# Small unused tiles in front of the activation tiles, hi and lo halves joined

## The chip, the cores and the metric

The kernel runs on one core of a Trainium2 chip. The metric is the device time of one execution in microseconds: 1652.95 us, the median of 3 runs (1650.94 to 1655.68).

## The reference

Two blocks are applied to x, 256 positions by 1024 channels, all in float32. The first has two layers. Each layer is a half-weighted SwiGLU FFN, a mixer, and a second such FFN:

```python
for l in range(DEPTH):                                   # DEPTH = 2
    x = x + 0.5 * swiglu(rms_norm(x, ffn1_norm[l]), ffn1_w_gate_up[l], ffn1_w_down[l])
    u = rms_norm(x, mix_norm[l]) @ w_in[l]
    y = concatenate([ssd_mixer(u_ssd), mlstm_mixer(u_ml), rwkv7_mixer(u_rw)])
    x = x + y @ w_out[l]
    x = x + 0.5 * swiglu(rms_norm(x, ffn2_norm[l]), ffn2_w_gate_up[l], ffn2_w_down[l])
return rms_norm(x, final_norm)
```

The hidden width of an FFN is 2816. The second block has one layer: attention of 8 heads with a distance bias beside a short convolution, an output projection, and a fifth FFN of the same size with a three-tap convolution on its up projection; six modulation vectors come from a 1024 x 6144 product with a condition vector (the "ada" weights).

## The kernel before

Channels lie on the partitions, positions along them: an activation is a tile of [128, 8, 256] (8 blocks of 128 channels, 256 positions each). A weight matrix is cut into blocks of 128 x 128; 7 blocks are one chunk of 448 KB in the order in which they are used. `fetch` (line 120) brings a chunk into `raw` through SyncE's DMA queue, six ahead. `chunk` (lines 125 to 135) splits it: ScalarE casts it to float32r (`whi`, line 133) and VectorE subtracts (`wlo`, line 134); four chunks of each are held. Activations are split in the same way (`split`, lines 203 to 205). So one float32 block product is three matmuls of 256 columns, hi x hi, hi x lo, lo x hi (`mm`, lines 150 to 154), summed in a PSUM bank `d`:

```python
PE.matmul(p, h, xh, ...)      # line 152
PE.matmul(p, h, xl, ...)      # line 153
PE.matmul(p, lo, xh, ...)     # line 154
```

The first argument after `p` is the 128 x 128 weight block, which TensorE loads; the second is the activation, which streams through it. There are 3808 blocks, 11424 such matmuls.

The stages run in this order: FFN, mixers, FFN in layer 0; the same in layer 1; attention and fifth FFN. In an FFN the up projection (`group`, `dense2`: 8 blocks per result) reads `xn`, the normalised x, and the down projection (22 blocks per result) reads the hidden tiles `hh` and `hl`. The first four results of an up projection, the "lead", read `xg` instead, x times the gain without the normalisation, so that TensorE has work while the statistic is computed (sum on TensorE, line 220; root on GpSimd, line 211; spread over partitions on TensorE, line 249). In the mixers the input projections read `xn` and a planner (`weave`) puts the chains of the three mixers between them in a fixed order; then `w_out` reads their results `y`. TensorE, ScalarE, VectorE and GpSimd each work in the order of the program.

The tiles that matter here come from pools. `big` (line 255) is [128, 8, 256], 8192 bytes of each partition, four buffers: `xg`, `xn`, the SSD part's inputs and its result each take two of them, one for hi and one for lo. The small results of the mixers take [128, 2, 256] tiles `w2` of a ring. The hidden tiles `hh` and `hl` (lines 314, 315) are the first large tiles of a pool per FFN. Where a tile begins follows from what was allocated before it. In the built program, before and after the change, the tiles begin at these byte offsets of a partition, modulo 512 (one weight block is 512 bytes, one activation block 1024). The weights, `whi` and `wlo`, begin at 416 in every buffer and every block, before and after. The columns d give the activation's offset minus 416, modulo 512.

| moving operand | matmuls | offset before | d before | offset after | d after |
|---|---|---|---|---|---|
| `xn` of five FFNs | 4800 | 416 | 0 | 96 | 192 |
| `xn` and SSD result in two mixers | 2160 | 416 | 0 | 96 | 192 |
| `xg`, six leads | 576 | 416 | 0 | 352 | 448 |
| `xn` of the attention | 480 | 416 | 0 | 352 | 448 |
| mixers' `y` in `w2` tiles | 384 | 192 | 288 | 96 | 192 |
| hidden, FFN 1 of layer 0 | 528 | 96 | 192 | 96 | 192 |
| hidden, FFN 2 of layer 0 | 528 | 96 | 192 | 352 | 448 |
| hidden, FFN 1 of layer 1 | 528 | 96 | 192 | 160 | 256 |
| hidden, FFN 2 of layer 1 | 528 | 224 | 320 | 32 | 128 |
| hidden, fifth FFN | 528 | 224 | 320 | 288 | 384 |
| `mixed` of the attention | 192 | 224 | 320 | 96 | 192 |
| `xgh` and `xgl`, two leads of 258 columns | 192 | 96, 160 and on in steps of 8 | 192, 256 and on | 224, 288 and on | 320, 384 and on |

Of the kernel before, what the change touches and what calls it, by code (L numbers as in the profile page):

```python
# [16 lines left out]
T = 256  # L17
# [22 lines left out]
DENSE = 0.34  # L40
W_OUT = ((("rwkv0", "rwkv1"), (12, 13, 14, 15)), (("ssd",), (0, 1, 2, 3, 4, 5, 6, 7)), (("mlstm",), (8, 9, 10, 11)))
# [35 lines left out]
def _program(tc, a, order, dbg=None):  # L77
# [91 lines left out]
    def group(mat, l, ms, K, xs, lead):  # L169
        pp = [bank(), bank()]  # L170

        def step(i, m, k):
            mm(pp[i // 2][:, i % 2], (mat, l, k, m), xs[0][:, k], xs[1][:, k], k == 0 and i % 2 == 0, k == K - 1)
# [107 lines left out]

    OUTS = ((0, 1), (2, 3), (4, 5), (6,), (7,))
# [4 lines left out]
    def gained(js, xg, gain):  # L287
        col = [P(gain, j) if isinstance(gain, str) else gain[:, j:j + 1] for j in js]
        for j, c in zip(js, col):
            S.activation(xg[0][:, j, :T], x[:, j], AF.Copy, scale=c)  # L290
        for j, c in zip(js, col):
            V.scalar_tensor_tensor(xg[1][:, j, :T], x[:, j], c, xg[0][:, j, :T].bitcast(F32),
# [7 lines left out]
    def normalize(rb, gain):  # L300
        xn = pair()
        for j in range(0, DT, 2):
# [3 lines left out]
            split(n, xn[0][:, j:j + 2], xn[1][:, j:j + 2])  # L306
        return xn

    def ffn(l, which, acc, xg, next_gain):
        with tc.tile_pool(name=f"ffn{which}{l}", bufs=1) as fp:  # L310
            gu, dn = f"ffn{which}_w_gate_up", f"ffn{which}_w_down"
            rb, = stat_rstd([acc], D, EPS)
            xn = normalize(rb, f"ffn{which}_norm{l}")
            hh = fp.tile([128, FT, T], F32R, name="hh")
            hl = fp.tile([128, FT, T], F32R, name="hl")
            groups = ADA[2 * l + which - 1]
            n_ada = 8 * len(groups)
            for t in range(FT):
# [15 lines left out]
                split(h, hh[:, t], hl[:, t])  # L334
# [16 lines left out]
            for js in OUTS:  # L351
                p = dense2(dn, l, js, FT, (hh, hl))[:, :len(js)]
# [20 lines left out]
    def mixers(l, acc, xg):  # L373
# [10 lines left out]

        nka = mp.tile([128, 4], F32, name="nka")
# [30 lines left out]
        def w_in(name):  # L416
# [37 lines left out]
        def w_out(js, ks, last):  # L454
            p = bank()[:, :len(js)]
            for u, j in enumerate(js):
                for i, k in enumerate(ks):
                    hi, lo = b["y", k]
                    mm(p[:, u], ("w_out", l, k, j), hi, lo, i == 0, i == len(ks) - 1)
# [1025 lines left out]
```

## Time and profile before

| what | value |
|---|---|
| median of 3 runs | 1652.95 us (1650.94 to 1655.68) |
| the profiled execution: span from first to last instruction | 1648.7 us |
| TensorE matmul / weight load busy | 1606.0 us (97%) / 1540.1 us (93%) |
| VectorE / ScalarE / GpSimd busy | 1162.8 us (71%) / 1001.7 us (61%) / 46.3 us (3%) |
| read from HBM | 287.51 MB, 175 GB/s over the span |

Matmuls are pipelined, so the busy time of TensorE counts overlapping instructions once and says little of its pace; the distance between the starts of two matmuls (here: the pitch) is read from the timeline, or from the count of matmuls in a stretch. A line such as `d<-big,whi` gives the output tile, then the inputs by the program's names without buffer numbers. An activation is named there by its pool's name: `big` is `xn` or `xg` or the SSD result, `w` is a tile of the ring `w2`.

### The profile page before, as it was taken

How to read it: one execution, taken by the hardware profiler on the slowest of the kernel's cores; microseconds unless marked ns; L12 is line 12 of the kernel's file. 1: busy time of each engine (PE TensorE's matmuls, PEld its weight loads, DVE VectorE, ACT ScalarE, POOL GpSimd, SP SyncE). 2: the span in 40 equal slices, each digit the busy share in tenths (PEclk: the TensorE clock that was granted, in tenths of full speed). 3: DMA queues.
4: the chain of work that ended last, by engine and by line, in shares of the span. 5: the costliest groups of instructions: out<-in, count | busy, mean ns of one | idle time of the engine just before them, and what ended most of it. 6: DMA issues, size and time to landing. Idle time of an engine off the chain costs nothing.

```text
span 1648.7 us, 33731 instructions
## 1 busy us (share of the span) xinstructions
PE 1606.0 (97%) x13660; PEld 1540.1 (93%) x13660; DVE 1162.8 (71%) x1961; ACT 1001.7 (61%) x1688; POOL 46.3 (3%) x58
## 2 busy tenths in 40 slices
PE   8999999999999999999999899999999999999998
PEld 7999988877999999999998887899999998999997
DVE  7755689856877655777568975588785676698863
ACT  6444586887655444544457788766544566477753
POOL 0000001000000000000000100000000000000000
PEclk9999999999999999999999999999999999999999
DMA  7855643334357656597563333435885553455562
GB/s 257 291 182 188 200 128 123 104 116 125 112 175 253 212 181 194 180 328 241 183 200 126 123 102 106 129 126 200 290 294 180 185 163 112 146 165 183 184 195 73
DMA packets 106717, 290.81 MB, mean 176 GB/s; under 512 B 15640, under 2 KB 28096, under 8 KB 106432
## 3 DMA queue, kind: packets, MB, share of 16 engines
q1 hardware_dynamic: 106272, 288.12, 53.7%
q8 instruction: 107, 1.75, 0.4%
q10 hardware_dynamic: 288, 0.52, 0.1%
q14 instruction: 50, 0.41, 0.1%
HBM read 287.51 MB, written 1.09 MB: 175 GB/s over the span
## 4 chain that ended last, share of the span: by engine, by line
PE 80%; issue 13%; ACT 3%; DVE 3%; POOL 1%; DMA 0%; DVEq 0%; POOLq 0%; SPq 0%; ACTq 0%
PE d L154 22%; PE d L153 22%; PE d L152 22%; PE m L680 1%; POOL stm L211 1%; PE m L743 1%; PE m L1055 1%; ACT whi L133 1%; PE m L1059 1%; PE m L725 1%; DVE wlo L134 1%; PE st L220 1%; PE m L694 1%; PE m L1057 1%; PE m L590 0%
## 5 line engine op out<-in xcount | busy, mean ns | idle before, releaser
L134 DVE TENSOR_TENSOR wlo<-raw,whi 128x896 fp32r<-128x896 f32 x544 | 590.9, 1089 | 266.8 <-ACT whi L133 264.7
L152 PE MATMUL d<-big,whi 128*128 128x256 f32 x2672 | 761.6, 285 | 3.6 <-ACT whi L133 2.2
L154 PE MATMUL d<-big,wlo 128*128 128x256 f32 x2672 | 762.1, 285 | 1.8 <-DVE wlo L134 1.8
L153 PE MATMUL d<-big,whi 128*128 128x256 f32 x2672 | 762.4, 285 | 0.2
L133 ACT CAST whi<-raw 128x896 fp32r<-128x896 f32 x544 | 511.3, 942 | 389.2 <-PE d L153 281.4
L152 PEld LDWEIGHTS d<-big,whi 128*128 128x128 f32 x2672 | 512.8, 192 | 12.8 <-issue 6.3
L154 PEld LDWEIGHTS d<-big,wlo 128*128 128x128 f32 x2672 | 512.6, 192 | 6.8 <-issue 2.5
L153 PEld LDWEIGHTS d<-big,whi 128*128 128x128 f32 x2672 | 512.9, 192 | 3.8 <-issue 1.7
L153 PE MATMUL d<-hl,whi 128*128 128x256 f32 x880 | 244.5, 278 | 0.0
L152 PE MATMUL d<-hh,whi 128*128 128x256 f32 x880 | 244.1, 277 | 0.0
L154 PE MATMUL d<-hh,wlo 128*128 128x256 f32 x880 | 243.8, 277 | 0.0
L154 PEld LDWEIGHTS d<-hh,wlo 128*128 128x128 f32 x880 | 165.2, 188 | 0.0
L152 PEld LDWEIGHTS d<-hh,whi 128*128 128x128 f32 x880 | 165.2, 188 | 0.0
L153 PEld LDWEIGHTS d<-hl,whi 128*128 128x128 f32 x880 | 165.1, 188 | 0.0
L204 ACT CAST hh<-h 128x256 fp32r<-128x256 f32 x88 | 35.4, 406 | 71.0 <-DVE h L333 71.0
L1115 DVE SCALAR_TENSOR_TENSOR adasum<-ada,sc,adasum 128x1024 f32<-128x1024 f32 x42 | 53.9, 1282 | 13.9 <-DMA ada<-ada 13.8
L332 ACT ACTIVATE s<-d 128x256 f32<-128x256 f32 x80 | 30.6, 382 | 30.0 <-PE d L154 29.9
L205 DVE TENSOR_TENSOR hl<-h,hh 128x256 fp32r<-128x256 f32 x88 | 36.8, 422 | 15.3 <-ACT hh L204 14.5
L1148 DVE SCALAR_TENSOR_TENSOR up<-raw,par,up 128x255 f32<-128x255 f32 (+1 forms) x88 | 37.2, 479 | 11.1 <-ACT raw L1144 10.8
L333 DVE TENSOR_TENSOR h<-s,d 128x256 f32<-128x256 f32 x88 | 36.1, 416 | 5.1 <-ACT s L332 5.1
L211 POOL TENSOR_TENSOR stm<-stm,mhalf 128x2 f32<-128x2 f32 (+1 forms) x14 | 15.1, 1079 | 818.3 <-DVE stm L237 591.0
L154 PE MATMUL d<-w,wlo 128*128 128x256 f32 x128 | 37.0, 289 | 0.0
(402 smaller groups left out, 1845.0 us busy)
## 6 DMA issues: line engine op xcount, KB each, us to landing
raw<-ws SPq DMA_DIRECT2D x544, 448.0 KB, 3.8
ada<-ada SPq DMA_DIRECT2D x48, 512.0 KB, 6.1
w<-da SPq DMA_DIRECT2D x16, 256.0 KB, 5.4
w<-small SPq DMA_DIRECT2D x10, 256.0 KB, 3.8
ab<-abias SPq DMA_DIRECT2D x1, 1536.0 KB, 8.5
x<-xT SPq DMA_DIRECT2D x4, 256.0 KB, 5.2
w<-da SPq DMA_DIRECT2D x8, 128.0 KB, 3.6
w<-dw SPq DMA_DIRECT2D x4, 256.0 KB, 5.4
```

The source lines that it names most:

```text
L133: S.copy(hi, raw)
L134: V.tensor_sub(lo, raw, hi.bitcast(F32))
L152: PE.matmul(p, h, xh, start=start, stop=False, skip_group_check=True)
L153: PE.matmul(p, h, xl, start=False, stop=False, skip_group_check=True)
L154: PE.matmul(p, lo, xh, start=False, stop=stop, skip_group_check=True)
L204: S.copy(hi, src)
L205: V.tensor_sub(lo, src, hi.bitcast(F32))
L211: G.tensor_tensor(dst, m, mhalf.to_broadcast([128, n]), op=OP.pow)
L332: S.activation(s, p[:, 0], AF.Silu)
L333: V.tensor_mul(h, s, p[:, 1])
L1115: V.scalar_tensor_tensor(acc, w, sc[:, k:k + 1], acc, op0=OP.mult, op1=OP.add)
L1148: V.scalar_tensor_tensor(dst[:, i, d:], raw[:, i, :T - d], P(w, 3 * j + k), dst[:, i, d:], op0=OP.mult, op1=OP.add)
```

## The change

A new helper `gap` allocates a tile of a given number of bytes in a pool and fills it with zeros on GpSimd; nothing reads it. It moves every tile that is allocated after it. The table `GAPS` gives the bytes: before `xg`, before `xn`, at the head of the mixers' pool, before the hidden tile of each FFN, and before the attention's `mixed` tiles. The hi and lo halves, until now two tiles, become one tile with a leading index: `pair` (two names, `pair0` and `pair1`, used in turn), `hp` for the hidden values, `m0` and `m1`, and one `w2` tile for the hi and lo of each 128 channels of a mixer's result. `publish` therefore splits the two halves of its result one at a time. The numbers of matmuls, of weight blocks and of DMAs stay the same.

```diff
+GAPS = {"xg": 448, "xn": 192, "mix": 288, "ffn": (384, 128, 448, 192, 448), "attn": 256}
...
     def dense(p, mat, l, m, K, xs, k0=0):
         for k in range(K):
-            mm(p, (mat, l, k0 + k, m), xs[0][:, k], xs[1][:, k], k == 0, k == K - 1)
+            mm(p, (mat, l, k0 + k, m), xs[:, 0, k], xs[:, 1, k], k == 0, k == K - 1)
...
-    def big(dtype=F32R):
-        return act.tile([128, DT, T], dtype, name="big", bufs=4)
-
-    def pair():
-        return big(), big()
+    turn = []
+
+    def gap(pool, n):
+        if n:
+            turn.append(0)
+            G.memset(pool.tile([128, n // 4], F32, name=f"gap{len(turn)}"), 0.0)
+
+    pairs = []
+
+    def pair(dtype=F32R):
+        pairs.append(0)
+        return act.tile([128, 2, DT, T], dtype, name=f"pair{len(pairs) % 2}")
...
     def ffn(l, which, acc, xg, next_gain):
         with tc.tile_pool(name=f"ffn{which}{l}", bufs=1) as fp:
             gu, dn = f"ffn{which}_w_gate_up", f"ffn{which}_w_down"
+            gap(fp, GAPS["ffn"][2 * l + which - 1])
+            hp = fp.tile([128, 2, FT, T], F32R, name="hp")
             rb, = stat_rstd([acc], D, EPS)
             xn = normalize(rb, f"ffn{which}_norm{l}")
-            hh = fp.tile([128, FT, T], F32R, name="hh")
-            hl = fp.tile([128, FT, T], F32R, name="hl")
...
-                split(h, hh[:, t], hl[:, t])
+                split(h, hp[:, 0, t], hp[:, 1, t])
...
+        gap(mp, GAPS["mix"])
         nka = mp.tile([128, 4], F32, name="nka")
...
-                if i == 0:
-                    b["sz"] = big(F32)
...
-                    b["xs"] = big(F32)
+                    zx = pair(F32)
+                    b["xs"], b["sz"] = zx[:, 0], zx[:, 1]
...
     def publish(b, k, o, ring):
-        yh, yl = ring(128, 2, T, dtype=F32R), ring(128, 2, T, dtype=F32R)
-        split(o, yh, yl)
         for j in range(2):
-            b["y", k + j] = yh[:, j], yl[:, j]
+            y = b["y", k + j] = ring(128, 2, T, dtype=F32R)
+            split(o[:, j], y[:, 0], y[:, 1])
...
             xn = modulate(rb2, a1[:, 0], mod[:, 0:8])
-            mixed = [[mp.tile([128, 4, T], F32R, name=f"m{h}{i}") for h in "hl"] for i in range(2)]
+            gap(mp, GAPS["attn"])
+            mixed = [mp.tile([128, 2, 4, T], F32R, name=f"m{i}") for i in range(2)]
...
             rb, = stat_rstd([acc], D, EPS)
             xn = modulate(rb, a1[:, 1], mod[:, 24:32])
-            hh = fp.tile([128, FT, T], F32R, name="hh")
-            hl = fp.tile([128, FT, T], F32R, name="hl")
+            gap(fp, GAPS["ffn"][4])
+            hp = fp.tile([128, 2, FT, T], F32R, name="hp")
...
-    acc, xg = new_acc(), pair()
+    acc = new_acc()
+    gap(act, GAPS["xg"])
+    xg = pair()
+    gap(act, GAPS["xn"])
```

Two places show instructions that are new in an engine's order. The first is GpSimd at the start, through the first FFN into the first mixers; `stm` is the mean square whose root is taken, `vn` and `kkst` belong to mLSTM and RWKV. Before:

```order
L211 TENSOR_TENSOR stm<-stm,mhalf 128x2
L866 MEMSET vn 128x4 x2
L211 TENSOR_TENSOR stm<-stm,mhalf 128x2
L211 TENSOR_TENSOR kkst<-kkst,mhalf 128x8
L600 MEMSET w_3039 128x512
```

and now:

```order
L261 MEMSET gap_88 128x112
L261 MEMSET gap_91 128x48
L261 MEMSET gap_153 128x96
L212 ISA
L212 TENSOR_TENSOR stm<-stm,mhalf 128x2
L261 MEMSET gap_2471 128x72
L876 MEMSET vn 128x4 x2
L212 TENSOR_TENSOR stm<-stm,mhalf 128x2
L212 TENSOR_TENSOR kkst<-kkst,mhalf 128x8
```

Three memsets stand ahead of all else, and one stands ahead of the `vn` memsets and the root at the head of the mixers; the later stages have one each in the same place.

The second is ScalarE in the first mixers, where `publish` casts the first RWKV result (line 204 before, 205 now); `R` is RWKV's, `nat` SSD's. Before:

```order
L1046 ACTIVATE w_4323<-w_4323 128x512
L1067 ACTIVATE w_4317<-big 128x512
L204 CAST w_4457<-w_4409 128x512
L745 COPY w_4303<-m 64x256
L361 ACTIVATE w_4535<-d,par 128x256 x2
L362 COPY w_4534<-d 128x512
```

and now:

```order
L1055 ACTIVATE w_4325<-w_4325 128x512
L1076 ACTIVATE w_4319<-pair_3252 128x512
L205 CAST w_4459<-w_4411 128x256
L205 CAST w_4462<-w_4411 128x256
L373 ACTIVATE w_4539<-d,par 128x256 x2
L374 COPY w_4538<-d 128x512
L756 COPY w_4305<-m 64x256
```

One cast of 512 columns became two of 256, and RWKV's copy moved two places back, behind the convolution's first steps.

## Rows read from the trace of the kernel before

**Rows 1.** The page, part 1: busy time, share of the span, instructions.

```profile
span 1648.7 us, 33731 instructions
...
PE 1606.0 (97%) x13660; PEld 1540.1 (93%) x13660; DVE 1162.8 (71%) x1961; ACT 1001.7 (61%) x1688; POOL 46.3 (3%) x58
```

**Rows 2.** Timeline of TensorE, up projection, first FFN: start us, us, engine, line.

```profile
59.85 0.28 PE L153 MATMUL d<-big,whi 128*128 128x256 f32 x1
59.97 0.28 PE L154 MATMUL d<-big,wlo 128*128 128x256 f32 x1
60.09 0.28 PE L152 MATMUL d<-big,whi 128*128 128x256 f32 x1
```

**Rows 3.** Timeline of TensorE, down projection, first FFN.

```profile
159.78 0.28 PE L152 MATMUL d<-hh,whi 128*128 128x256 f32 x1
159.89 0.28 PE L153 MATMUL d<-hl,whi 128*128 128x256 f32 x1
160.01 0.28 PE L154 MATMUL d<-hh,wlo 128*128 128x256 f32 x1
160.12 0.28 PE L152 MATMUL d<-hh,whi 128*128 128x256 f32 x1
```

**Rows 4.** Windows, matmuls into `d`: stretch, length, busy (count), clock, DMA, GB/s.

```profile
40.00:120.00 80.00, 80.00 (x669) 1.00 0.71 241
690.00:780.00 90.00, 89.48 (x744) 1.00 0.81 280
1470.00:1560.00 90.00, 89.90 (x749) 1.00 0.58 182
145.00:190.00 45.00, 45.00 (x399) 1.00 0.62 193
610.00:655.00 45.00, 45.00 (x399) 1.00 0.61 194
800.00:845.00 45.00, 45.00 (x400) 1.00 0.61 194
1265.00:1310.00 45.00, 45.00 (x385) 1.00 0.58 185
1577.00:1590.00 13.00, 13.00 (x113) 1.00 0.62 197
1594.50:1607.50 13.00, 13.00 (x117) 1.00 0.61 201
466.00:474.00 8.00, 8.00 (x70) 1.00 0.51 177
```

**Rows 5.** The page, part 5: the largest matmul group.

```profile
L152 PE MATMUL d<-big,whi 128*128 128x256 f32 x2672 | 761.6, 285 | 3.6 <-ACT whi L133 2.2
```

**Rows 6.** Windows, every engine: PE, PEld, DVE, ACT, POOL busy.

```profile
230.00:355.00 125.00, 116.26 (x1175) 104.73 (x1173) 101.85 (x234) 100.50 (x168) 11.33 (x16) 1.00 0.39 119
1470.00:1560.00 90.00, 89.90 (x749) 89.70 (x748) 76.86 (x141) 70.35 (x125) 0.00 (x0) 1.00 0.58 182
```

**Rows 7.** Windows, matmuls into `d` in the first mixers.

```profile
230.00:355.00 125.00, 74.48 (x556) 1.00 0.39 119
```

**Rows 8.** Waits of TensorE: total us, times, longest.

```profile
PE st L249 <- POOL stm L211: 8.4, 8, 1.7
```

**Rows 9.** Instructions of line 204 (`split`, ScalarE): count, min/median/max ns.

```profile
L204 ACT CAST hh<-h x88: 399/406/410, 31.0 to 1263.8; 128x256 fp32r<-128x256 f32 x88
...
L204 ACT CAST w<-w x4: 606/612/618, 373.2 to 1074.9; 128x512 fp32r<-128x512 f32 x4
```

**Rows 10.** Instructions of line 205 (`split`, VectorE).

```profile
L205 DVE TENSOR_TENSOR hl<-h,hh x88: 415/421/427, 31.4 to 1264.9; 128x256 fp32r<-128x256 f32 x88
...
L205 DVE TENSOR_TENSOR w<-w,w x4: 684/688/694, 374.3 to 1075.5; 128x512 fp32r<-128x512 f32 x4
```

**Rows 11.** Groups on GpSimd: busy us, mean ns, idle before, releaser.

```profile
L805 POOL MEMSET w<- 128x256 f32 x2 | 0.6, 312 | 51.4 <-DVE w L653 51.4
L866 POOL MEMSET vn<- 128x4 f32 x4 | 0.3, 106 | 370.2 <-PE d L154 370.2
```

More of the change, by code (lines that the diff above doesn't have):

```diff
@@ L172, in step @@
         def step(i, m, k):
-            mm(pp[i // 2][:, i % 2], (mat, l, k, m), xs[0][:, k], xs[1][:, k], k == 0 and i % 2 == 0, k == K - 1)
+            mm(pp[i // 2][:, i % 2], (mat, l, k, m), xs[:, 0, k], xs[:, 1, k], k == 0 and i % 2 == 0, k == K - 1)
         for i, m in enumerate(ms):
@@ L280, in add_square, with halves @@
             V.tensor_add(a, a, acc[:, 1:2])
+    def halves(t):
+        return t if isinstance(t, list) else (t[:, 0], t[:, 1])
     OUTS = ((0, 1), (2, 3), (4, 5), (6,), (7,))
@@ L288, in gained @@
         col = [P(gain, j) if isinstance(gain, str) else gain[:, j:j + 1] for j in js]
+        hi, lo = halves(xg)
         for j, c in zip(js, col):
-            S.activation(xg[0][:, j, :T], x[:, j], AF.Copy, scale=c)
+            S.activation(hi[:, j, :T], x[:, j], AF.Copy, scale=c)
         for j, c in zip(js, col):
-            V.scalar_tensor_tensor(xg[1][:, j, :T], x[:, j], c, xg[0][:, j, :T].bitcast(F32),
+            V.scalar_tensor_tensor(lo[:, j, :T], x[:, j], c, hi[:, j, :T].bitcast(F32),
                                    op0=OP.mult, op1=OP.subtract)
@@ L305, in normalize @@
                 V.scalar_tensor_tensor(n[:, i - j], x[:, i], P(gain, i), rb, op0=OP.mult, op1=OP.mult)
-            split(n, xn[0][:, j:j + 2], xn[1][:, j:j + 2])
+            split(n, xn[:, 0, j:j + 2], xn[:, 1, j:j + 2])
         return xn
@@ L351, in ffn @@
             for js in OUTS:
-                p = dense2(dn, l, js, FT, (hh, hl))[:, :len(js)]
+                p = dense2(dn, l, js, FT, hp)[:, :len(js)]
                 V.scalar_tensor_tensor(cut(x, js), p, 0.5, cut(x, js), op0=OP.mult, op1=OP.add)
@@ L457, in w_out @@
                 for i, k in enumerate(ks):
-                    hi, lo = b["y", k]
-                    mm(p[:, u], ("w_out", l, k, j), hi, lo, i == 0, i == len(ks) - 1)
+                    mm(p[:, u], ("w_out", l, k, j), b["y", k][:, 0], b["y", k][:, 1], i == 0, i == len(ks) - 1)
             V.tensor_add(cut(x, js), cut(x, js), p)
@@ L1077, in ssd @@
         yield "o2"
-        yh, yl = pair()
+        y = pair()
         for j in range(0, 8, 2):
@@ L1082, in ssd @@
             dbg(f"ssd_y{l}_{j // 2}", xs[:, j:j + 2])
-            split(xs[:, j:j + 2], yh[:, j:j + 2], yl[:, j:j + 2])
+            split(xs[:, j:j + 2], y[:, 0, j:j + 2], y[:, 1, j:j + 2])
             for i in (j, j + 1):
-                b["y", i] = yh[:, i], yl[:, i]
+                b["y", i] = y[:, :, i]
             yield 2.0
@@ L1216, in mixed_norm @@
                 rb, = stat_rstd([q[:, 0:2]], 512, EPS)
-                hi, lo = mixed[i]
+                hi, lo = halves(mixed[i])
                 src = (at, cv)[i]
@@ L1240, in half @@
                     for k in range(4):
-                        mm(p[:, u], ("w_out_2", 0, 4 * i + k, j), mixed[i][0][:, k], mixed[i][1][:, k],
+                        mm(p[:, u], ("w_out_2", 0, 4 * i + k, j), mixed[i][:, 0, k], mixed[i][:, 1, k],
                            first and u == 0 and k == 0, last and k == 3)
@@ L1277, in second @@
                 V.tensor_mul(vg[:, 0], vg[:, 0], vg[:, 1])
-                split(vg[:, 0], hh[:, t], hl[:, t])
+                split(vg[:, 0], hp[:, 0, t], hp[:, 1, t])
             acc = new_acc()
             for js in OUTS:
-                p = dense2("w_down_2", 0, js, FT, (hh, hl))
+                p = dense2("w_down_2", 0, js, FT, hp)
                 for u, j in enumerate(js):
@@ L1292, in second @@
         r = stat_cols([acc], D, EPS)
-        o = big(F32).rearrange("p j (t i) -> p (j t i)", t=2)
+        o = pair(F32)[:, 0].rearrange("p j (t i) -> p (j t i)", t=2)
         for t in range(2):
```

13 lines of the change are left out of this document (6 added, 7 removed).

## The prediction

> **What bounds the kernel now.** I read the page's busy shares first, then the groups by line, then the stretches of single stages, and last single matmuls in order of time. The reader should see in the busy shares that TensorE is at 97% of a 1648.7 us span, VectorE at 71%, ScalarE at 61% [rows 1]. That share alone says little, since each matmul of the largest group is booked with 285 ns [rows 5] while the next one starts long before. What counts is the distance from start to start. In the stream that reads `big`, starts are 120 ns apart; in the stream that reads `hh`/`hl` they are 110 to 120 ns apart, as far as two decimals tell [rows 2, 3]. To measure it over a stage, divide a stretch by its matmuls. A matmul is counted if any of its 0.28 us lies in the stretch, so the pitch is (length + 0.28) / count. This gives [rows 4]:
>
> - `big` as moving operand, up projections: 80.28/669 = 120.0 ns, 90.28/749 = 120.5 ns (the 744 in 90 us has ada work between).
> - `hh`/`hl`, down projections of the first three FFNs: 45.28/399 = 113.5 ns twice, 45.28/400 = 113.2.
> - The same loop in the fourth FFN: 45.28/385 = 117.6 ns. In the fifth: 13.28/113 = 117.5 ns, and a few us later 13.28/117 = 113.5 ns.
> - `w2` (the mixers' outputs): 8.28/70 = 118.3 ns.
>
> All of these are the same instruction: 128x128 weights, 256 float32r columns, granted clock 1.00 in every row, so the 2.4 GHz level. Line, count and the work of the other engines do not sort them. The byte offset does (table in the section on the kernel). Write d for moving offset minus weight offset, modulo 512 bytes. d = 0 has 120; d = 192 has 113.5; d = 320 has 117.6, or 113.5 for a while; d = 288 has 118.3. The strongest evidence is the down projection: one loop, one set of neighbours, 113.5 at d = 192 and 117.6 at d = 320. So TensorE bounds the FFNs, and its pitch depends on where the operand lies. `big` is read by 3 x 2672 = 8016 of 11424 dense matmuls [rows 5], all at d = 0.
>
> **The change, part by part.** By its new addresses, 6960 of the 8016 (`xn` and the SSD output, now `pair0`) go to d = 192, a distance that the trace has seen in three FFNs. The other 1056 (`xg` and the attention's `xn`, now `pair1`) go to d = 448, unseen.
>
> 1. `xn` in five FFNs, 5 x 960 = 4800 matmuls: 120.0 - 113.5 = 6.5 ns each, 31.2 us. TensorE has no idle worth naming in these stretches (busy 80.00 of 80, 89.90 of 90 [rows 4]), so all of it is on the path. What is late next: DMA at 280 GB/s and a share of 0.81 would need 280 x 120/113.5 = 296 GB/s, share 0.86; still room. In the fifth FFN VectorE is busy 76.9 of 90 us, ScalarE 70.4 [rows 6]; the 90 us become 85.1, so 90% and 83%. I count no loss; if that stage cannot follow at all, 960 x 6.5 = 6.2 us are lost.
>
> 2. The mixers, 2160 matmuls of `pair0` and 384 of `w2` (d = 288 before, 192 now). Per layer 1080 + 192. In 230 to 355 us TensorE has work for 116.3 of 125 us [rows 6], so it waits for chains on ScalarE and VectorE; 556 dense matmuls lie there [rows 7], worth 3.6 us. A shorter stream in front of a wait only lengthens the wait; I take a third, 1.2 us. The remaining 716 run almost without waits: 524 x 6.5 = 3.4 us and 192 x (118.3 - 113.5) = 0.9 us. So 5.5 us a layer, 11.0 in all; bounds 4 (a quarter) and 15.8 (everything).
>
> 3. `pair1` at d = 448. The seven windows with d other than 0 have a mean of 115.3 ns; no row is nearer, since 0 (120) and 320 (117.5) stand on either side. Bounds 113.5 and 120. The attention's 480 matmuls: 480 x 4.7 = 2.3 us, bounds 0 and 3.1. The six leads on `xg` (6 x 96 matmuls) are followed by a wait of TensorE for the statistic's root, 8.4 us over 8 times [rows 8]: that chain sets the end, not the lead. Counted 0, bound 3.7 us.
>
> 4. The hidden tiles `hp`, 528 matmuls in each FFN: d goes 192, 192, 192, 320, 320 to 192, 448, 256, 128, 384. The first stays. The second and third leave 113.5 for something unseen, the fourth leaves 117.6, the fifth about 116 (between its two windows). At 115.3: +1.9, -1.2, -0.4, together +0.3 us. Bounds: all at 113.5, -3.5 us; all at 120, +6.9 + 1.3 + 2.1 = +10.3 us.
>
> 5. The `mixed` tiles, 192 matmuls, d = 320 before as in the fourth FFN, 192 now: 192 x 4.1 = 0.8 us.
>
> 6. `publish` splits each half by itself: four times two casts of 406 ns in place of one of 612, and two subtractions of 421 in place of one of 688 [rows 9, 10]: 0.2 us more on ScalarE and 0.15 on VectorE each time. In the mixers after 355 us TensorE does not wait for them (it is at `xm`, `z` and `w_out` work); 0, at most 4 x 0.35 = 1.4 us.
>
> 7. Ten memsets of 32 to 112 columns on GpSimd, each between 106 ns (4 columns) and 312 ns (256 columns) [rows 11]. Seven of them wait for the whole stage before, as the `vn` memsets already do (370 us behind `PE d L154` [rows 11]). Behind them on GpSimd stands the root of the next statistic, and this needs the same last matmul plus an addition to x, a square, a sum and a scaling. So the memset is done first: 0. Without this cover 7 x 0.3 = 2 us.
>
> Sum: -31.2 - 11.0 - 2.3 + 0.3 - 0.8 = -45.0 us. The span goes from 1648.7 to 1603.7. The median of the runs, 1652.95, is 4.25 above this execution's span; I carry that over: **1608 us**.
>
> A rule speaks against all this. The Trainium skill (SBUF — State Buffer, "Who interferes with whom") states: "PE and ACT never wait on anyone." Its page TensorE: Matmul & The Clock Gate ("Step-by-step: what each phase is for") says that loading the next weights takes no read bandwidth from the running matmul, and ("Back-to-back issue gap") puts 256 columns at 256/2.4 + 2.5 = 109.2 ns, an estimate from that page. By these an offset inside the partition changes nothing. The trace disagrees: 113.5 and 117.6 ns in one loop at two offsets [rows 4], and 109.2 in no window.
>
> **The rivals.**
>
> *The second level.* At d = 320 the fifth FFN runs at 117.5 ns, then at 113.5 after two transposes came between its matmuls [rows 4]: the offset alone does not fix the pitch, the phase in which two matmuls follow does too. If `pair0` falls into such a level, the gain is 120.0 - 117.5 = 2.5 ns: 12.0 us in the FFNs, some 3.8 in the mixers, and the second and third `hp` lose 528 x 4.0 x 2 = 4.2. Together -11.6: 1641 us. For it: the mixers interrupt the stream often. Against it: three FFNs at d = 192 show 113.2 to 113.5.
>
> *Nothing changes.* The offset is not the cause, or the tiles do not land where I think; the added work is hidden: 1653 us. The rule just cited gives this. Against it stands the one loop at two offsets.
>
> *Slower.* The 120 ns belongs to the up projections, not to the offset, and stays; only the down projections answer to the offset, and their new distances are as bad as 0. Then item 4 at its upper bound decides alone: 1653 + 10.3 = 1663 us. It decides where the `xn` stretches still show 119 ns or more and the second to fifth down projections over 118. For it: 120 appears only where `big` is read, never in a down projection. Against it: 4.1 of the 6.5 ns are seen inside the down loop itself, from 113.5 to 117.6.
>
> **How the numbers follow.** My forecast 0.78, the second level 0.10, nothing changes 0.06, slower 0.06. The forecast's own bounds: best -31.2 - 15.8 - 3.1 - 3.7 - 3.5 - 0.8 = -58.1, so 1595; worst -31.2 - 4 - 0.8 + 10.3 + 6.2 = -19.5, so 1633. That range holds its 0.78 and I leave the rest out. What this kernel can tell from no change is 0.3%, 5 us. Forecast and second level are both faster by more: 0.88; the same 0.06; slower 0.06.
>
> **What would show it.** Item 1: stretches of an up projection with 113 to 114 ns, that is 705 to 710 matmuls in 80 us instead of 669. Item 2: the mixers' part shorter by 5 to 6 us each with TensorE's idle time there larger. Items 3 and 4: the pitch of each `hp` and of the attention, each at its own distance. Item 7: no new wait of the statistic's root on GpSimd. I am wrong if the `xn` stretches keep 119 ns or more, if a level of 117 to 118 appears there, or if a stretch is at 113.5 and TensorE waits for the weights' split instead.

## The result and the profile after

The changed kernel takes 1625.03 us (median of 4 runs, 1623.02 to 1627.10), the kernel before beside it 1654.32 (1650.94 to 1659.03): a ratio of 0.9825, interval 0.9802 to 0.9849. Forecast were 1608 us in a range of 1595 to 1633, and a span shorter by 45 us. The span is shorter by 23.4: 1648.7 [rows 1] against 1625.3. The profiled execution itself took 1627.1 us, the longest of the four. The median lies 17 us above the forecast and 16 us below the 1641 us of the rival *the second level*, so the time alone does not choose between the two; the pitches of single stages do.

The page of after, part 1 (busy time, share of the span, instructions):

```profile
span 1625.3 us, 33775 instructions
...
PE 1584.9 (98%) x13660; PEld 1516.4 (93%) x13660; DVE 1161.4 (71%) x1965; ACT 1000.1 (62%) x1692; POOL 47.5 (3%) x68
```

Single matmuls of the first up projection, from the timeline of after (start us, us, engine, line):

```profile
59.98 0.28 PE L155 MATMUL d<-pair,wlo 128*128 128x256 f32 x1
60.09 0.28 PE L153 MATMUL d<-pair,whi 128*128 128x256 f32 x1
```

They keep their 0.28 us; the starts have moved from 120 ns apart [rows 2] to 110, as far as two decimals tell. Stretches of after, matmuls into `d` alone (stretch, length, busy (count), clock, DMA share, GB/s), to lay beside [rows 4]:

```profile
40.00:120.00 80.00, 80.00 (x708) 1.00 0.77 252
690.00:720.00 30.00, 30.00 (x267) 1.00 0.87 309
1460.00:1550.00 90.00, 90.00 (x766) 1.00 0.62 190
145.00:190.00 45.00, 45.00 (x399) 1.00 0.64 193
605.00:650.00 45.00, 45.00 (x399) 1.00 0.64 194
790.00:835.00 45.00, 45.00 (x378) 1.00 0.59 184
1255.00:1300.00 45.00, 45.00 (x381) 1.00 0.61 182
1385.00:1397.00 12.00, 12.00 (x108) 1.00 0.53 171
```

By (length + 0.28) / count: up projections at d = 192 at 113.4 ns (rows one and two) but 117.9 in the fifth FFN (row three). Hidden tiles: 113.5 at 192 and at 448, 119.8 at 256, 118.8 at 128. The attention's `pair1` at 448 stands at 113.7 in the last 12 us of its stage, but its first 96 matmuls were at 117.8; its mean is 115.3. The same instruction at the same clock has several paces here, and which one it takes follows d, except that 192 and 448 show two.

Where the 23.3 us come from, each stage from its first dense matmul to the next stage's first, in us:

```
stage                          before    after   change   forecast
up, FFNs 1 to 4                470.74   447.39   -23.36    -25.0
up, fifth FFN                  115.54   113.80    -1.75     -6.2
mixers, input part, layer 0    208.75   212.63    +3.89  |
mixers, input part, layer 1    208.76   208.18    -0.58  |  -11.0
mixers, outputs (two layers)   105.80   104.30    -1.51  |
attention, input part           79.39    77.62    -1.76     -2.3
attention, output part          26.96    24.98    -1.98     -0.8
leads                                             -1.05      0
down, FFN 1 and 2 of layer 0   120.44   120.40    -0.04  |
down, FFN 1 of layer 1          60.22    63.71    +3.49  |  +0.3
down, FFN 2 of layer 1          62.55    63.02    +0.47  |
down, fifth FFN                 73.42    74.35    +0.93  |
```

So the up projections paid nearly as forecast, and three things fell short of the forecast by 22 us together: the mixers (12.8), the fifth FFN's up (4.5), three hidden tiles (4.6). For the mixers, here are windows with every engine (PE, PEld, DVE, ACT, POOL busy, clock, DMA share, GB/s): first the input part of layer 0 in before, then of both layers in after, and last two stretches inside after's layer 0.

```profile
213.00:421.70 208.70, 199.36 (x1799) 175.02 (x1797) 154.93 (x326) 163.99 (x288) 14.22 (x18) 1.00 0.38 118
```

```profile
209.00:421.60 212.60, 203.01 (x1787) 177.25 (x1786) 153.92 (x328) 163.41 (x289) 14.79 (x18) 0.95 0.38 115
862.00:1070.00 208.00, 198.95 (x1792) 174.53 (x1791) 153.57 (x333) 164.50 (x294) 14.80 (x18) 0.98 0.39 117
...
228.80:239.00 10.20, 9.72 (x37) 6.80 (x36) 7.51 (x16) 7.78 (x14) 1.77 (x3) 0.50 0.26 87
...
290.40:297.20 6.80, 6.80 (x117) 6.15 (x117) 3.70 (x12) 6.05 (x10) 0.00 (x0) 1.00 0.75 247
```

The granted clock was 1.00 throughout this part in before and 0.95 and 0.98 in after: here it falls to 0.50, the 1.2 GHz level, for 20.5 us in layer 0 (four falls) and 10.2 in layer 1 (three). The timeline of TensorE shows what came before the first of them and what it does to a matmul:

```profile
225.08 0.28 PE L153 MATMUL d<-pair,whi 128*128 128x256 f32 x1
226.51 1.05 PE L556 MATMUL m<-cst,w 128*128 128x2 f32 x8 [1.16 <-ACT w L551]
227.42 0.36 PE L154 MATMUL d<-pair,whi 128*128 128x256 f32 x1
...
228.88 0.40 PE L154 MATMUL d<-pair,whi 128*128 128x256 f32 x1
229.07 0.42 PE L155 MATMUL d<-pair,wlo 128*128 128x256 f32 x1
```

TensorE waited 1.16 us for ScalarE, worked again for some 2 us, and from 228.8 its starts are 0.2 us apart in place of 0.113. The second and third fall follow waits of 1.4 and 2.4 us. The fourth, at 297.2 us, does not: ahead of it (last row above) TensorE was busy all the time, with 117 matmuls, of which 14 went into `d` and the others were small ones of the chains. The waits of TensorE that grew in this part, total, times, longest, before and then after:

```profile
PE m L680 <- issue: 3.2, 2, 1.9
PE m L545 <- ACT w L540: 1.4, 2, 0.8
```

```profile
PE m L691 <- issue: 3.8, 2, 2.4
PE m L556 <- ACT w L551: 2.5, 2, 1.4
```

Line 680 of before is line 691 of after, 545 is 556. That they grew because the dense matmuls ahead of them end earlier and the chains do not is the likely reason, but not tested. All waits of TensorE in the part together fell, from 10.8 to 9.5 us.

The attention's output part shows the same thing the other way round, before and then after:

```profile
1418.80:1446.00 27.20, 25.76 (x205) 25.26 (x203) 18.66 (x30) 13.83 (x22) 1.42 (x1) 0.94 0.50 160
```

```profile
1398.20:1424.00 25.80, 24.17 (x208) 23.59 (x207) 19.17 (x31) 14.39 (x23) 1.42 (x1) 1.00 0.56 176
```

Here before had a fall to 0.50, for 3.4 us, and after had none.

### The profile page after: what moved, and what is told of

Its sections match the earlier page's. It is cut to its first block, busy times and chain, and to the rows that moved or that the text cites. A ratio compares the mean times of both kernels' runs of the same rounds, so it can differ in the third digit from the quotient of the medians.

```text
span 1625.3 us, 33775 instructions
## 1 busy us (share of the span) xinstructions
PE 1584.9 (98%) x13660; PEld 1516.4 (93%) x13660; DVE 1161.4 (71%) x1965; ACT 1000.1 (62%) x1692; POOL 47.5 (3%) x68
## 3 DMA queue, kind: packets, MB, share of 16 engines
q8 instruction: 107, 1.75, 0.4%
## 4 chain that ended last, share of the span: by engine, by line
PE 77%; issue 13%; DVE 5%; ACT 2%; DMA 1%; POOL 1%; SPq 0%; DVEq 0%; POOLq 0%; ACTq 0%
PE d L155 21%; PE d L153 21%; PE d L154 21%; DVE wlo L135 1%; DMA ada<-ada 1%; PE m L691 1%; PE m L754 1%; PE m L1064 1%; POOL stm L212 1%; PE m L1068 1%; PE m L736 1%; PE st L221 1%; PE m L705 1%; ACT whi L134 1%; PE m L1066 1%
## 5 line engine op out<-in xcount | busy, mean ns | idle before, releaser
L153 PE MATMUL d<-pair,whi 128*128 128x256 f32 x2672 | 753.2, 282 | 4.8 <-ACT whi L134 2.1
L155 PE MATMUL d<-pair,wlo 128*128 128x256 f32 x2672 | 753.8, 282 | 1.8 <-DVE wlo L135 1.8
L154 PE MATMUL d<-pair,whi 128*128 128x256 f32 x2672 | 752.9, 282 | 0.1
L153 PEld LDWEIGHTS d<-pair,whi 128*128 128x128 f32 x2672 | 508.8, 190 | 14.8 <-issue 5.9
L155 PEld LDWEIGHTS d<-pair,wlo 128*128 128x128 f32 x2672 | 508.1, 190 | 7.2 <-DVE wlo L135 2.9
L154 PEld LDWEIGHTS d<-pair,whi 128*128 128x128 f32 x2672 | 508.5, 190 | 3.0 <-issue 1.4
L154 PE MATMUL d<-hp,whi 128*128 128x256 f32 x880 | 246.6, 280 | 0.0
L155 PE MATMUL d<-hp,wlo 128*128 128x256 f32 x880 | 246.1, 280 | 0.0
L153 PE MATMUL d<-hp,whi 128*128 128x256 f32 x880 | 246.1, 280 | 0.0
L155 PEld LDWEIGHTS d<-hp,wlo 128*128 128x128 f32 x880 | 166.2, 189 | 0.0
L154 PEld LDWEIGHTS d<-hp,whi 128*128 128x128 f32 x880 | 166.1, 189 | 0.0
L153 PEld LDWEIGHTS d<-hp,whi 128*128 128x128 f32 x880 | 166.1, 189 | 0.0
L206 DVE TENSOR_TENSOR hp<-h,hp 128x256 fp32r<-128x256 f32 x88 | 36.7, 421 | 15.3 <-ACT hp L205 14.5
L1157 DVE SCALAR_TENSOR_TENSOR up<-raw,par,up 128x255 f32<-128x255 f32 (+1 forms) x88 | 37.2, 480 | 10.6 <-ACT raw L1153 10.3
L344 ACT ACTIVATE s<-d 128x256 f32<-128x256 f32 x80 | 30.2, 378 | 23.3 <-PE d L155 22.2
L154 PE MATMUL d<-w,whi 128*128 128x256 f32 x128 | 37.1, 290 | 0.0
```

The costliest lines, as they stand in the source:

```text
L153: PE.matmul(p, h, xh, start=start, stop=False, skip_group_check=True)
L154: PE.matmul(p, h, xl, start=False, stop=False, skip_group_check=True)
L155: PE.matmul(p, lo, xh, start=False, stop=stop, skip_group_check=True)
L206: V.tensor_sub(lo, src, hi.bitcast(F32))
L344: S.activation(s, p[:, 0], AF.Silu)
L1157: V.scalar_tensor_tensor(dst[:, i, d:], raw[:, i, :T - d], P(w, 3 * j + k), dst[:, i, d:], op0=OP.mult, op1=OP.add)
```

## The experiments

Several edits shift the `gap` tiles so that chosen tiles change their distance while the others keep theirs.

**The up projections' tile back at 0.** All else as changed (one tile for hi and lo, order, hidden tiles; one memset more).

```diff
-GAPS = {"xg": 448, "xn": 192, "mix": 288, "ffn": (384, 128, 448, 192, 448), "attn": 256}
+GAPS = {"xg": 448, "xn": 512, "mix": 480, "ffn": (576, 320, 128, 192, 448), "attn": 256, "later": 192}
...
+            gap(later, GAPS["later"])
```

> The changed kernel with its joined tiles, gaps and split publish, but pair0 put back at distance 0 from the weights (512 bytes of gap instead of 192; the later gaps adjusted so that every other distance is as in the changed kernel). Theory (the distance between moving operand and weights sets the pitch): the up projections go back to 120 ns (669 matmuls in 80 us) and 117 to 118 us each, the mixers' input part back to 208.8 us without half-clock stretches, the whole to 1649 us of span, ratio 1.00 to before. Rival (joining hi and lo, or the order of the tiles, made the gain): up projections stay at 113.5 ns and 111.5 to 112.5 us, the span near 1625.

Measured: 1650.48 us, ratio to before 0.9975 (0.9964 to 0.9987). A stretch of the first up projection, matmuls into `d`:

```profile
40.00:120.00 80.00, 80.00 (x669) 1.00 0.72 238
```

The up projections are at 120.0 ns again, with the very count of before [rows 4]. With every other part of the change left in, nearly the whole gain is gone: the distance carries it. The mixers' input parts did not come out as expected: 209.9 and 209.7 us, with the clock at 0.50 for 10.2 and 6.8 us of them.

**The offset alone.** Before's separate tiles, `big` moved to d = 192 by an unused tile ahead of it; six more at the head of the later pools keep `hh`, `w2` and the rest where they were.

```diff
+            if not later: gap(fp, 320)
...
+        gap(mp, 320)
...
-    acc, xg = new_acc(), pair()
+    acc = new_acc()
+    gap(act, 192)
+    xg = pair()
...
+            gap(later, 320)
```

> The kernel before with one gap of 192 bytes ahead of the big tiles (distance 0 becomes 192 for all of xg, xn and the SSD result) and gaps of 320 bytes at the head of the later pools, so that all other tiles keep their distance. hi and lo stay separate tiles, publish is not split. Theory: the first four up projections lose 5.7 to 6.1 us each, the fifth 2 to 6 by the level it falls into, the leads and the attention some 3 together, the mixers' input part changes by -5 to +4 with its half-clock stretches; the span is 1618 to 1626. Rival (joining is needed): no change, 1649. Rival (the gain of the changed kernel came with the hidden tiles or the publish): no more than 5 us.

Measured: 1624.75 us, 0.9832 (0.9795 to 0.9869): the same gain without joined tiles. But its up projections did not agree among themselves, and the first three of them gained 2.5, 2.5 and 3.7 us in place of the 5.7 to 6.1 expected. Three stretches, one of the first FFN and two within one stage of the third:

```profile
40.00:120.00 80.00, 80.00 (x682) 1.00 0.74 245
700.00:725.00 25.00, 25.00 (x215) 1.00 0.92 329
740.00:775.00 35.00, 35.00 (x312) 1.00 0.75 246
```

117.7, 117.6, then 113.1 ns, all at d = 192. The offset opens two levels, from here on the lower (113.3 ns) and the upper (117.8); it does not choose between them.

**The weights moved instead.** The activations keep their places modulo 512, the weights move by 320 bytes.

```diff
+    G.memset(wp.tile([128, 80], F32, name="gapw"), 0.0)
+    G.memset(act.tile([128, 48], F32, name="gapa"), 0.0)
```

> The kernel before with the weights' tiles moved by 320 bytes and the activations by 512, so that every activation keeps its offset modulo 512 and only the weights lie elsewhere: big at distance 192, the hidden tiles of the first three FFNs at 384, of the last two and the attention's mixed tiles at 0. Theory (only the distance counts): up projections at 113.5 ns (the fifth perhaps 117.8), the first three down projections at 118 to 119 ns and 62.5 to 63 us in place of 60.2, the last two at 120 ns; span about 1637. Rival (the place of the moving operand alone counts): nothing changes, 1649, down projections at 113.5 ns.

Measured: 1640.54 us, 0.9913 (0.9885 to 0.9940). The up stages went from 120.0 to 113.4 to 115.9 ns as stage means; the down stages, now at 384 and 0, from 113.4 and 117.8 to 118.7 and 120.0. So no absolute place counts, only the distance between the two operands. Besides TensorE, ScalarE and VectorE touch the weights' tiles: they write the next blocks there, at the same offset. They are not the cause, since in before's first up projection the pitch is 120.0 ns where one of them writes weights meanwhile (757 matmuls) and 119.9 where none does (190). What is left is TensorE's own loading of weights beside its stream; how the two meet no run shows.

**A scan with the hidden tiles**, which are free to move one by one.

```diff
-GAPS = {"xg": 448, "xn": 192, "mix": 288, "ffn": (384, 128, 448, 192, 448), "attn": 256}
+GAPS = {"xg": 448, "xn": 192, "mix": 288, "ffn": (224, 256, 288, 224, 288), "attn": 256}
```

This puts the five hidden tiles at d = 32, 64, 96, 160 and 224.

> The changed kernel with other gaps ahead of the five hidden tiles: distances 32, 64, 96, 160 and 224 in the five down projections in order of time. Theory (the pitch repeats with 256 bytes and is good at odd multiples of 64): 113.5 ns (or its upper level 117.8) at 64 only, 117 to 119 ns at the other four. Rival (only distances close to 0 and 256 are bad): 113.5 ns at 64, 96 and 160, more at 32 and 224. Down projections of 113.5 ns last 60.2 us in the first four FFNs, of 118.7 ns 63.0.

Measured (one run): 1632.85 us. Matmuls into `d` in the first four down stages, d = 32, 64, 96, 160:

```profile
145.00:190.00 45.00, 45.00 (x388) 1.00 0.62 191
605.00:650.00 45.00, 45.00 (x385) 1.00 0.59 185
795.00:840.00 45.00, 45.00 (x377) 1.00 0.59 184
1260.00:1305.00 45.00, 45.00 (x386) 1.00 0.61 187
```

Stage means 116.7, 117.8, 120.0, 117.3; the fifth, d = 224, 118.3. That 96 is as slow as 0 was expected by neither theory nor rival. With the values above the pace of the FFN stages repeats every 256 bytes wherever both places were seen: 0 and 256 at 120.0, 128 and 384 at 118.7, odd multiples of 64 at 113.3 or 117.8. Of the others 32, 160 and 224 lie between, and 96 is at 120.0. The mixers' `y` at 288 in before, with other matmuls in between, had 117.5 as a mean, not quite the 116.7 of 32. In this run the third and second FFN's up, at an unchanged d = 192, stood at the upper level and the fifth's at the lower, other than in after.

**The same kernel once more**, the changed one with nothing edited.

> The changed kernel, unchanged, profiled once more. Theory (the level of a run of matmuls at an odd multiple of 64 is drawn at its start): some up stages swap levels, at 113.3 to 113.6 or 117.5 to 118 ns, so the span lies within 1617 to 1640 us, and the tiles at 128, 256 and 384 repeat their pitch within 0.3 ns. Rival (the level is set by the address or the program): every stage has its pitch within 0.3 ns again, the fifth FFN's up at 117.8.

Measured: 1635.41 us (one run, span 1633.6). First the first and the fifth FFN's up, matmuls into `d`:

```profile
40.00:120.00 80.00, 80.00 (x682) 1.00 0.74 244
1470.00:1550.00 80.00, 80.00 (x708) 1.00 0.61 189
```

117.7 and 113.4 ns, the reverse of after. The tiles at 128 and 256 repeated theirs to 0.1 ns. In the second FFN the level changed in the middle of a stage. The timeline of TensorE there:

```profile
540.73 0.28 PE L154 MATMUL d<-pair,whi 128*128 128x256 f32 x1
540.84 0.32 PE L155 MATMUL d<-pair,wlo 128*128 128x256 f32 x1
541.00 0.28 PE L153 MATMUL d<-pair,whi 128*128 128x256 f32 x1
```

One matmul started 0.05 us late (0.16 after its forerunner); ahead of it the stage ran at 113.3, behind it at 117.8.

**Interruptions on purpose.** Unused transposes, 1 to 4 of them, at four places of each up stage.

```diff
+BREAKS = (6, 10, 14, 18)
...
+    def breaks(t, hp):
+        if t in BREAKS:
+            q = mps(tag="st")
+            for i in range(BREAKS.index(t) + 1):
+                PE.transpose(q[:, i * 128:i * 128 + 128], hp[:, 0, t - 2, 0:128].bitcast(F32), ident)
```

> The changed kernel with 1, 2, 3 and 4 transposes of a 128x128 block of hp (results unused, into the st bank) between the output tiles of every FFN's up stage, ahead of t = 6, 10, 14 and 18. Theory (at a distance of 192 a run of matmuls falls into one of two levels, 113.3 or 117.8 ns, when it starts, and keeps it until something interrupts it): the level changes at some of the 20 interruptions and nowhere else within an uninterrupted run; up stages lie between 110.5 and 117 us plus at most 1.5 us for the transposes, and no longer at all 113.3 or all 117.8. Rival 1 (the level is set per stage, by the tile or by the other engines' load): each stage keeps one level through its interruptions. Rival 2 (the level drifts): it changes at places without an interruption.

Measured (one run): 1634.5 us. In the first up projection the transposes lie at 47.0, 69.7, 91.9 and 114.0 us. Matmuls into `d` before the first, and behind the first, the second and the third:

```profile
30.00:46.00 16.00, 16.00 (x144) 1.00 0.69 222
48.00:68.00 20.00, 20.00 (x172) 1.00 0.87 307
71.00:76.50 5.50, 5.50 (x51) 1.00 0.72 243
93.00:113.00 20.00, 20.00 (x178) 1.00 0.65 189
```

113.1, 117.9, 113.3, 113.9 ns. The level changed at 8 of the 20 interruptions. Elsewhere it changed once, in the fifth FFN, behind a wait of TensorE of 0.46 us at 1462 us, and never within an uninterrupted run of matmuls. Rivals 1 and 2 fall. Which level follows is not an even draw: after four transposes it was the lower five times of five, and near the end of the up stages of the first four FFNs, behind the small matmuls of the "ada" product, it was the lower in 33 of the 36 stages of the nine profiles with `xn` at 192.

**All hidden tiles at 192.**

```diff
-GAPS = {"xg": 448, "xn": 192, "mix": 288, "ffn": (384, 128, 448, 192, 448), "attn": 256}
+GAPS = {"xg": 448, "xn": 192, "mix": 288, "ffn": (384, 384, 384, 256, 256), "attn": 256}
```

> The changed kernel with all five hidden tiles hp at 192 bytes from the weights (after has them at 320, 320, 256, 128 or 384 from theirs; by the distance mod 512 they ran at 113.3, 113.3, 120.0, 118.7 and 118.8 ns). Theory (the distance sets the pitch; odd multiples of 64 give 113.3 or 117.8): third FFN's down 63.71 -> 60.2 us, fourth's 63.0 -> 60.2, or 62.5 each at the upper level, fifth's 74.35 -> 72 to 73.5; first two stay at 60.2 (or 62.5); total 1625 -> 1618 us, with both levels possible 1615 to 1627. Rival (the down stages are set by their evictions or by the slot of the tile in the pool): no down stage moves by over 0.5 us.

The changed kernel's hidden tiles lie at 192, 448, 256, 128 and 384 from the weights, as in the table of the section on the kernel, not at the distances that the expectation gives.

Measured: 1617.24 us (1612.54 to 1620.61), 0.9783 (0.9756 to 0.9809), faster than before and as expected; the changed kernel's four executions, taken at another time, lie above all four of these. The third and fourth down take 60.20 us in place of 63.71 and 63.02, the fifth 72.17 in place of 74.35. The third, matmuls into `d`, 113.5 ns:

```profile
785.00:830.00 45.00, 45.00 (x399) 1.00 0.66 194
```

**The up projections' tile at 64** (also an odd multiple of 64), on top of this.

```diff
-GAPS = {"xg": 448, "xn": 192, "mix": 288, "ffn": (384, 384, 384, 256, 256), "attn": 256}
+GAPS = {"xg": 448, "xn": 576, "mix": 416, "ffn": (512, 512, 512, 384, 256), "attn": 256, "later": 128}
...
+            gap(later, GAPS["later"])
```

> x5_hp192 with the xn pair of the FFNs and mixers at 64 bytes from the weights in place of 192, hp at 192 but for the fourth FFN's at 320 (64 mod 256). So far, down stages at 192 or 448 (192 mod 256) all ran at 113.3 ns, and those at 64 or 320 at 117.8 (only parts of the fifth FFN's at 113); the up stages at 192 ran at either. Theory A (the two kinds of odd multiples of 64 differ: 192 mod 256 tends to the lower level, 64 mod 256 to the upper): the five up stages are at 117.5 to 118 ns over most of their length, 115.3 to 116.5 us (fifth 113.8), fourth down 62.5; span 1630 to 1640. Theory B (both have the same two levels, drawn at the start of each run): some up stages or parts of them at 113.3 to 113.6 as with 192, fourth down 60.2 or 62.5; span 1612 to 1632.

Measured (one run): 1641.98 us. Matmuls into `d`: first up (d = 64), first down (192), fourth down (320), and two stretches of the fifth down (192):

```profile
40.00:120.00 80.00, 80.00 (x682) 1.00 0.74 244
145.00:190.00 45.00, 45.00 (x384) 1.00 0.61 187
1265.00:1310.00 45.00, 45.00 (x385) 1.00 0.62 187
1587.00:1601.00 14.00, 14.00 (x121) 1.00 0.58 178
1604.50:1616.50 12.00, 12.00 (x109) 1.00 0.33 101
```

Theory A holds: all five up stages at 117.7. What was not expected: the down stages at 192, at 113.3 in the first four FFNs of every kernel until then, followed at 117.9. A reading that fits: a down stage begins without an interruption behind its up stage and keeps the level that it finds. In all other profiles the up stage ahead of a down stage at 192 or 448 had ended at the lower level, or at 120.0 with `xn` at 0, so this run is the only test of it. In the fifth FFN the stream dropped to 112.7 only after a break at 1602 us.

**Filling TensorE's waits in the mixers.**

```diff
+        fill(pst, kk.rearrange("p h t -> p (h t)"), 8)
...
+            if dst is Tm:
+                fill(pz0, et.rearrange("p i b s -> p (i b s)"), 20)
```

`fill` issues unused transposes, 8 ahead of line 556's matmuls and 20 ahead of line 691's.

> The changed kernel with unused transposes in TensorE's waits in the two mixers: 8 of kk ahead of the matmuls that fill kkst (line 556 of after), 20 of et ahead of the first-level matmuls on am (line 691 of after), twice a layer each. Theory (the granted clock falls to the 1.2 GHz level after the waits that the faster matmuls made longer, 20.5 us in the first mixer and 10.2 in the second, and that ate the mixers' gain): TensorE's wait before line 691's matmuls 2.4 -> under 0.7 us, at most one stretch at granted clock 0.5 per mixer, the in part of the mixers 212.6 and 208.2 -> 203 to 206 us each, total 1625 -> 1612 to 1618. Rival (the chain of VectorE and ScalarE sets the mixers' length): 208 to 213 us stay, with or without half clock, total 1624 to 1629.

Measured: 1666.2 us, 1.0079 (1.0053 to 1.0104), slower. Its first mixer's windows and waits:

```profile
211.00:436.00 225.00, 214.72 (x1843) 186.77 (x1843) 155.17 (x328) 161.10 (x287) 15.23 (x18) 0.96 0.35 109
```

```profile
PE m L211 <- DVE w L679: 3.5, 1, 3.5
```

The waits of line 691 went and stood ahead of the transposes themselves (L211, 3.5 us), TensorE is busy for 11.7 us more, and the clock still fell, for 17.1 us. This did not test what it was to test. The part became 12.4 us longer than in after, about what was added, so TensorE had no spare time at these two places.

**The planner's cost of a dense block adapted.** On the kernel with all hidden tiles at 192.

```diff
-DENSE = 0.34
+DENSE = 0.325
```

> x5_hp192 (all hidden tiles at 192) with the planner's cost of a dense block, DENSE, at 0.325 in place of 0.34, since the block has become some 4 per cent shorter; this moves small matmuls of the mixers' chains later among the dense ones, from about the third rwkv step on. Theory (the order was fitted to 120 ns, so TensorE now comes to the chains' matmuls too early and waits): the 2.4 us wait ahead of the first-level matmuls on am shrinks to under 1.8, half-clock stretches to 0 to 10 us a mixer, the in parts to 204 to 208 us, total 1608 to 1615. Rival (the waits are the chains' own lengths; another order only shifts them): in parts 208 to 213 as before, total 1615 to 1622.

Measured: 1625.94 us, 0.9815 (0.9783 to 0.9846), against 1617.24 without the edit. Input and output part of layer 0's mixers:

```profile
209.10:417.40 208.30, 196.50 (x1769) 170.87 (x1768) 151.25 (x319) 157.70 (x279) 14.59 (x17) 0.98 0.39 117
417.40:475.50 58.10, 55.62 (x470) 54.69 (x469) 47.20 (x85) 35.36 (x74) 3.42 (x2) 1.00 0.44 137
```

Half-clock time is 6.8 us a layer, but the waits add up to 11.8 us, against 9.4 without the edit, and the outputs take 58.1 us in place of 52.2. The input parts (208.3 and 208.0 us) are as the rival expected: this order only shifts the waits. The total is 4 us above its range, with the outputs of the two layers 6 us longer each.

**Before once more.**

> The kernel before, unchanged, profiled once more. In its first profile no stretch inside the mixers had granted clock 0.5 and their in parts took 208.8 us each; in the nine mixers of other experiments so far with before's order or with the 120 ns pitch there were 3.4 to 10.2 us of it. Theory A (the falls need the changed kernel's order or pitch): again none, 208.7 to 208.9 us each, span 1648 to 1650. Theory B (the waits of before suffice too, and whether a fall follows is chance): 3.4 to 10.2 us of granted clock 0.5 in at least one mixer, and that mixer longer by 0.3 to 0.5 us for each us of it; span 1650 to 1656.

Measured: 1652.47 us (one run, span 1650.7). Input parts of both layers:

```profile
214.40:424.20 209.80, 200.84 (x1788) 176.49 (x1787) 154.41 (x326) 162.99 (x287) 15.65 (x18) 0.98 0.38 117
872.60:1081.30 208.70, 197.93 (x1788) 173.60 (x1787) 154.35 (x326) 162.79 (x287) 15.65 (x18) 1.00 0.38 118
```

Theory B: before has such falls too, 7.0 us in one of its four profiled mixers. That mixer was longer by 1.0 us, 0.15 for each us of half clock and not the 0.3 to 0.5 expected; its waits were 1.9 us shorter. In the four mixers of the changed kernel the falls were 20.5, 10.2, 10.2 and 20.5 us; with the tile back at 0, 10.2 and 6.8.

## Why the prediction was right and where it was wrong

**Right: the offset is the cause, and it counts relative to the weights.** Back at 0, the offset alone and the weights moved leave next to nothing for the joining, the order or an absolute place. The rule of the Trainium skill (SBUF — State Buffer, "Who interferes with whom"), by which TensorE waits on nobody, is about engines that meet at a port. That it gives no change here is the prediction's reading of it, and the runs disagree with this reading by 113.3 against 120.0 ns. The estimate of 109.2 ns by the Trainium skill (TensorE: Matmul & The Clock Gate, "Back-to-back issue gap"), which that section gives for an isolated matmul, was reached nowhere: 113.3 is the best of any stage. With 113.4 ns in the up projections the rivals *nothing changes* and *slower* fall.

**Item 1 (FFNs, -31.2; measured -25.1).** Four FFNs gave 5.8 of 6.24 us each. The fifth gave 1.75. How near this came has luck in it, since the levels differ from execution to execution: the same five stages gave 21.7 us in the repeat, 16.4 with the offset alone and 29.0 with all hidden tiles at 192. The loss allowed for there, that VectorE and ScalarE cannot follow, was not what limited it. The rival *the second level* was; of the five up stages in this execution, it held that one alone: in the repeat, in the scan and in the kernel with all hidden tiles at 192 it took 110.2 us with the same neighbours, 5.3 less than before. The step that failed is the one behind that rival's chance, "three FFNs at d = 192 show 113.2 to 113.5": these were three down stages that all fell into the lower level, not a proof that 192 has one level.

**Item 2 (mixers, -11.0; measured +1.8).** This step failed, outside its bounds (4 to 15.8 gained). In the input parts the pitch gave most of what was forecast, 4.9 of 6.5 ns: 119.6 to 114.7 as a mean over 888 dense matmuls of a layer's input part. The outputs gave 1.5 of the 4.3 us counted for them, since the last 234 of a layer's 384 matmuls there fell into the upper level, 117.8. What the step left out is the clock. Three terms, worked out for each input part, account for it: 888 times the change of pitch, the change of TensorE's waits, and half of the time at granted clock 0.5.

```
               pitch   waits   half of half-clock   sum    measured
after, mix 0    -4.4    -1.4    +10.2               +4.5     +3.9
after, mix 1    -4.2    -1.4     +5.1               -0.5     -0.6
back at 0       -0.0    -3.2     +5.1               +1.9     +1.2
before again     0.0    -1.9     +3.5               +1.6     +1.0
repeat, mix 1   -3.5    -2.1    +10.2               +4.6     +3.9
weights, mix 0  -4.7    +2.7     +1.7               -0.3     +0.7
```

The sums miss by up to 1.0 us, in these and in all other input parts but those with fills. So the pitch's gain is there and the half clock takes it back. The wait that the prediction named costs too: with the weights moved, where the clock fell for only 3.4 us, 2.7 of 4.7 us went into longer waits.

Why the clock falls more often is not shown. Of 49 falls in the input parts without fills, 36 follow waits of TensorE; the other 13 follow a stretch of small matmuls, like the one from 290.4 us above, in which it hardly waited. So longer waits alone can't be the account, and no run took the waits away: the fills moved them, and the planner's cost shifted them. With the tile back at 0 TensorE's order is after's, the longest waits of lines 556 and 691 are 0.9 and 1.9 us as against 0.8 and 1.9 in before, and there are falls too, so chance has a part. That the mixers gain nothing is no accident of one profile: the sixteen input parts with `xn` at 192 and without fills had 3.4 to 20.5 us of half clock and took 207.8 to 212.7 us (mean 209.7), those of before 208.7 to 209.8. With before's order and `xn` at 192 the half clock was 3.4 to 10.2 us (the offset alone, the weights moved), with after's order and `xn` at 0 10.2 and 6.8, in before 0, 0, 7.0 and 0. How much of the falls the quicker matmuls cause, how much the new order and how much is chance stays open.

**Item 3 (attention -2.3; measured -1.8; leads 0, measured -1.05).** Within the bounds. The distance 448 is 192 modulo 256 and has its two levels; the 115.3 ns that the forecast took for it, as a mean over other distances, is by luck also the mean of this stage. In the repeat the clock fell for 3.4 us here, and the part took 79.4 us as in before. The leads gained while TensorE's wait for the root on GpSimd fell from 8.4 us [rows 8]; the same row of after:

```profile
PE st L250 <- POOL stm L212: 5.9, 8, 1.2
```

**Item 4 (hidden tiles, +0.3; measured +4.85).** Mechanism right, size off: 115.3 ns for all unseen distances was a mean of unlike things. They are 113.3 (448), 120.0 (256), 118.7 (128) and 118.8 (384), inside the bounds given (-3.5 to +10.3). The third FFN's down lost 3.5 of it.

**Item 5 (`mixed`, -0.8; measured -2.0):** larger than forecast, but not by the tiles: before's fall of the clock in this part is missing in after (rows of the attention's output part above). Profiles with `mixed` at 192 and such a fall show 40.4 to 41.0 us for this part and the lead behind it, those without one 39.0, before 40.9. So the missing fall is worth some 1.6 us, and the new distances about 0.2.

**Items 6 and 7 (0): right.** No wait of TensorE in the mixers names `publish`'s casts; the ten memsets, 162 ns each in the mean, brought no wait for the root.

**The time around the span.** The forecast carried 4.25 us; the changed kernel's median lies 0.3 below its profiled span. In each listed execution the time is 1.8 us above the span, so the rest of the 4.25 says that before's profiled execution was a quick one; after's was the slowest of its four. Single executions of the changed kernel took 1623 to 1635, with other levels and other falls of the clock. The median's 29 us of gain and the span's 23 differ by this.

## What to carry to other kernels

When matmuls of one shape show different pitches at full clock, sort them by the byte distance between the moving operand and the weights within a partition, and move the tile that is read most before anything else; here 8016 of 11424 matmuls stood at the worst distance and one shift of 192 bytes gave 1.7%. Check every tile that the same edit drags along, as three of the five hidden tiles went to worse places, and the version with all at 192 is the best measured (0.9783). One profile does not tell the pace of such a place: read several executions, stage by stage. Where quicker matmuls meet chains of other engines, read the granted clock of that stage before counting the gain.

## What the runs showed of the hardware

- The pitch of 128x128 by 256 matmuls depends on the distance d, in the FFN stages with a period of 256 bytes as far as both places were seen: 120.0 ns at 0 and 256, 118.7 at 128 and 384, 113.3 or 117.8 at odd multiples of 64. Seen once each: 116.7 at 32, 120.0 at 96, 117.3 at 160, 118.3 at 224.
- At 192 and 448 both levels occur, are held for up to 96 us, and can change at an interruption, of which a matmul 0.05 us late was enough. At 64 and 320 nearly all stretches were at the upper level.
- One program in one placement differed by 12 us between executions (1623.0 to 1635.4; with the offset alone 1622.5 to 1634.4), and the changed kernel's two profiles show other levels and other falls of the clock.
- The granted clock fell to 0.50 inside the mixers, mostly after waits of TensorE of 0.7 to 2.4 us, but also after a stretch of mostly small matmuls without a wait; in before as in after, in some places of some executions only.
